# A decoder trunk on one core: the weights' low parts of the first pair of chunks and of two down-projection pairs are made by other engines, at other places

## The chip, the cores and the metric

The kernel runs on one core of a Trainium2 chip. The metric is the device time of one execution in microseconds; here it is the median of 3 runs, 1110.24 us (1109.77 to 1112.19). Lower is better. The profile is of one further execution, which took 1109.46 us; between the first and the last instruction that it shows lie 1107.7 us.

## The reference, cut to what matters

512 positions of width 1024 pass through two decoder layers: one with dilated sliding-window attention, one with forgetting attention, and after each attention a gated convolutional feed-forward network (FFN) of width 2816. All is in float32. The change touches only the FFN:

```python
def conv_ffn(xn, w_up, cw, cb, w_down):
    a = xn @ w_up                                   # 1024 -> 2 * 2816
    ap = jnp.pad(a, ((0, 0), (CONV_W - 1, 0), (0, 0)))
    a = sum(ap[:, j:j + T] * cw[j] for j in range(CONV_W)) + cb
    gate, val = jnp.split(a, 2, axis=-1)
    return (jax.nn.gelu(gate, approximate=True) * val) @ w_down
```

## The kernel before

**Splits.** TensorE multiplies in a rounded float32 format. To keep float32 precision, each operand is split in a high part (a cast) and a low part (the operand less its high part), and each product is three matmuls: high times high, high times low, low times high (`mm3`, lines 294 to 297; L295, L296 and L297 in the profile). So each weight tile of 128x1024 (512 KB, called `wraw` when loaded by the SP queue, L48) must be split before TensorE can use it. The high part is always a cast on ScalarE. The low part is made in one of three ways: `low` subtracts on VectorE (L740, L76, L837) or, with an argument, on GpSimd; `added` has ScalarE write the negative of the high part's tile (L743: a copy of the raw tile with scale -1 into the rounded format) and then GpSimd issue a transfer that adds the raw tile to it (L744). The transfer reads the raw tile until it has landed.

**The up-projection** goes by chunks of 128 gate and 128 value columns, 22 chunks. The chunks 4 to 19 go in eight pairs, `PAIRS = range(2, 10)`. A pair is computed by a scheme with seven products instead of eight (sums and differences of blocks of weights and of the input are multiplied). TensorE takes the products of a pair in the order A11, S2, S3, A12, S1, A22, S4, with the next pair's A11 between A22 and S4. Each product is 24 matmuls (2 column halves, 4 blocks, 3 parts). VectorE adds products in PSUM between them: `sums` (L1062, "csum") and `ends` (L1047, L1048).

The generator `prepare(p)` (L730) makes the seven weight operands of a pair. Each `next(steps)` in the main loop (L1053 and on) lets it go one step further, so the order of its steps against the loop's own lines is the order of the instructions in each engine's queue. `ga`, `va`, `vb` and `gb` are the four raw tiles of a pair. `s3` and `s2` are differences of them. `gb` is A12's operand as it is; later GpSimd overwrites it with `gb - s2` (L782), and that is S4's operand. For the first pair (p = 2) the low parts of A11, S3, A12, S1, A22 and S4 are all made by `added`; for the later ones A11, S2 and S3 are done by VectorE, A12 by GpSimd, S1, A22 and S4 by `added`. In the loop the rest of the pair's generator is run after S2's product (`for _ in steps: pass`): that rest is S4's cast and `added`. Then the next pair's generator begins with the cast of its A11, later its low part.

After S2's product `sums(s12, ...)` waits to read what S2 wrote, and A12's product writes to the same PSUM bank, so A12's first matmul waits for that addition. `keep_first` (L1040) copies A11's result to SBUF for the same sums.

After a chunk's products come bias (L657 or L670), two convolution taps (L664, VectorE), GELU (L689), the product of gate and value on GpSimd (L686, "hc"), and a transfer of the result to DRAM (L684).

**The down-projection** takes 11 pairs of the 22 chunks, also by a scheme with fewer products. Its operands are two weight tiles and one tile of activations (`dact`) per pair. `pair_sums` (L823 to L825) forms sums of activations, `pair_highs` casts the three tiles (L833), `pair_lows` subtracts (L837), and `mul_one` issues the matmuls ("acc"), which multiply in the order activation high by weight high, activation high by weight low, activation low by weight high. The preparation of pairs 0 to 2 is placed among the last chunks of the up-projection; `down` begins with the highs of pair 3.

Of the kernel before, what the change touches and what calls it, by code (L numbers as in the profile page):

```python
# [12 lines left out]
AF = mybir.ActivationFunctionType  # L13
ALU = mybir.AluOpType
# [13 lines left out]
PAIRS = range(2, 10)  # L28
# [87 lines left out]
def trunk_kernel(ctx, tc, x, norm_gains, w_qkv_a, w_o_a, w_q_b, w_o_b, kv_norm, w_kvf, b_f,  # L116
                 w_up, conv_w, conv_b, w_down, rope, out):
    nc = tc.nc
    act, dve, pool, pe, sp = nc.scalar, nc.vector, nc.gpsimd, nc.tensor, nc.sync
# [529 lines left out]
    def ffn(l, bd, cp, nxt, ahead):  # L649
# [11 lines left out]
        def shifted(c, banks, bb, s):  # L661
            ps, ch = banks[s], s * NF + c
            for n in (1, 2):
                dve.scalar_tensor_tensor(bb[:, s, n:], ps[:, :T - n], cp[:, 2 - n, ch:ch + 1], bb[:, s, n:],  # L664
                                         ALU.mult, ALU.add)
# [22 lines left out]
        def glu(c, bb):  # L688
            act.activation(bb[:, 0, :], bb[:, 0, :], AF.Gelu_apprx_tanh)  # L689
            gated.append((c, bb))  # L690

        def post(c, banks, between=None):
            product()
            glu(c, taps(c, banks, between))
# [35 lines left out]
        def prepare(p):  # L730

            first = p == PAIRS[0]

            def high(a, raw):
                w[a] = t8([128, 2, 1024], F32R, name="w")
                act.copy(w[a][:, 0], raw)  # L736
                W2[p, a] = w[a].rearrange("p s (k c) -> p s k c", k=4)

            def low(a, raw, engine=dve):
                engine.tensor_tensor(w[a][:, 1], raw, w[a][:, 0].bitcast(F32), ALU.subtract)  # L740

            def added(a, raw):
                act.activation(w[a][:, 1], raw, AF.Copy, scale=-1.0)  # L743
                pool.dma_start(w[a][:, 1], raw, accum_op=ALU.add)  # L744

            w = {}
            ga = grab(2)
            high("A11", ga)
            if first:
                added("A11", ga)  # L750
            yield
            if not first:
                low("A11", ga)
            yield
            va = grab(1)
            s3 = t4([128, 1024], name="wsum")
            dve.tensor_tensor(s3, ga, va, ALU.subtract)
            high("S3", s3)
            if first:
                added("S3", s3)  # L760
            yield
            vb = grab(1)
            dve.tensor_tensor(va, va, vb, ALU.add)
            yield
            s2 = t4([128, 1024], name="wsum") if first else ga
            dve.tensor_tensor(s2, va, ga, ALU.subtract)  # L766
            high("S2", s2)
            gb = grab(1)
            high("A12", gb)
            if first:  # L770
                added("A12", gb)
            yield
            low("S2", s2)
            if not first:
                low("A12", gb, pool)
            high("S1", va)
            added("S1", va)
            W.load(W.n_split + 2)
            yield
            if not first:  # L780
                low("S3", s3)
            pool.tensor_tensor(gb, gb, s2, ALU.subtract)  # L782
            high("A22", vb)
            added("A22", vb)
            W.load(W.n_split + 3)
            yield
            high("S4", gb)
            added("S4", gb)
            yield
# [15 lines left out]

        acts, one, two, raws, later2 = {}, {}, {}, {}, {}
        H = slice(0, 512), slice(512, 1024)
        a11, s1_, s3_, s2_ = (slice(i * 256, i * 256 + 256) for i in range(4))  # L810

# [13 lines left out]
            dve.tensor_tensor(k[:, s2_], k[:, s1_], k[:, a11], ALU.subtract)  # L825
            pool.dma_start(sD[j], k[:, s2_])

        def pair_highs(j):

            raws[j] = [*W.take(2), acts.pop(j)]  # L830
            one[j] = [t8([128, 2, 1024], F32R, name="w") for _ in range(3)]
            for w, r in zip(one[j], raws[j]):
                act.copy(w[:, 0], r)  # L833

        def pair_lows(j):
            for w, r in zip(one[j], raws.pop(j)):
                dve.tensor_tensor(w[:, 1], r, w[:, 0].bitcast(F32), ALU.subtract)  # L837

        def load_two(j):
# [150 lines left out]
        first = first_products(bd, 3)  # L990
# [12 lines left out]
        steps = prepare(PAIRS[0])  # L1003
# [48 lines left out]
        s1 = keep_first(banks)  # L1052
        for p in PAIRS:  # L1053
            nxt_steps = prepare(p + 1) if p + 1 in PAIRS else prepare_last()
            if p + 1 not in PAIRS:
                pair_load(0)
            o2, o3, o4 = [[b[i][:, h] for b in banks] for i, h in ((0, HI), (1, LO), (1, HI))]
            s17, s12 = (t2([128, 2, 256], name="csum") for _ in range(2))

            def sums(dst, os, src):  # L1060
                for q in range(2):
                    dve.tensor_tensor(dst[q] if isinstance(dst, list) else dst[:, q], os[q], src[:, q], ALU.add)  # L1062

            times(p, "S2", o2)
            ends(pend)
            for _ in steps:
                pass
            steps = nxt_steps
            next(steps)
            bbs = [biased(*pend[0][:2])]  # L1070
            if p + 1 in PAIRS:
                next(steps)
            times(p, "S3", o3, True)
            sums(s12, o2, s1)
            bbs += [biased(*e[:2]) for e in pend[1:]]
            product()
            next(steps)
            shifted(*pend[0][:2], bbs[0], 0)
            times(p, "A12", [b[0][:, LO] for b in banks])
            sums(s17, o3, s1)  # L1080
            next(steps)
            shifted(*pend[0][:2], bbs[0], 1)
            glu(pend[0][0], bbs[0])
            times(p, "S1", o2)
            product()
            next(steps)
            if len(pend) > 1:
                shifted(*pend[1][:2], bbs[1], 0)
            times(p, "A22", o3)
            sums(o4, o2, s17)  # L1090
            next(steps)
            if len(pend) > 1:
                shifted(*pend[1][:2], bbs[1], 1)
                glu(pend[1][0], bbs[1])
            if p + 1 in PAIRS:
                later = begin(p + 1)
            else:
                W.n_get += 4 * len(PAIRS)
                begun = W.get(), bank([128, T], name="up")
                up(*begun, range(4))  # L1100
            next(steps, None)
            times(p, "S4", o2)
            pend = [(2 * p + q, banks[q], q, s1, s12) for q in range(2)]
            if p + 1 in PAIRS:
                banks, s1 = later, keep_first(later)
# [6 lines left out]
        ends(pend)  # L1112
        product()
        glu(pend[0][0], taps(*pend[0][:2]))
        pair_highs(1)
        up(W.get(), banks[1], range(KD))
        post(*pend[1][:2])
        pair_sums(2)
# [4 lines left out]
        glu(before[0], taps(*before, lambda: pair_lows(1)))  # L1123
        up(W.get(), banks[1], range(KD))
        before = NF - 1, banks
        post(*before)
        pair_highs(2)
        pair_sums(3)
        pair_lows(2)
        product()  # L1130
        pool.dma_start(hD[NF - 1], hc.pop(NF - 1))

# [513 lines left out]
    first, second = bd2.order[:2], bd2.order[2:]  # L1646
# [212 lines left out]
    for n in range(N + 3):  # L1859
        live = n < N  # L1860
        if live:
            j, i = units[n]
# [98 lines left out]
```

## Time and profile before

| | |
|---|---|
| median of 3 runs | 1110.24 us (1109.77 to 1112.19) |
| the profiled execution | 1109.46 us |
| its span, first to last instruction | 1107.7 us |
| mean granted clock of TensorE | 0.994 |
| TensorE busy | 1084.8 us (98%) |
| VectorE busy | 886.9 us (80%) |
| ScalarE busy | 699.7 us (63%) |
| GpSimd busy | 316.4 us (29%) |

A row of the timeline gives start, duration, engine, line of the code, operation, and what is written from what; in brackets the engine's idle time before it and what ended that. Engines: PE is TensorE, DVE is VectorE, ACT is ScalarE, POOL is GpSimd, SPq the queue of SP, which issues most loads. A row of the list of waits gives who waited for whom: microseconds in total, how many times, the longest. A row of the chain gives start, length and what the time went to. A row of the windows gives the stretch, its length, the busy time of PE, of weight loads, DVE, ACT and POOL, then TensorE's granted clock as a share of full speed, the share of the DMA engines' time, and GB/s. The two FFNs run the same code; the first pair of chunks lies near 222 us and near 806 us.

### The profile page before, as it was taken

The page shows a single profiled execution, that of the slowest core. Times are in us where ns is not written, and L with a number is a line of the kernel's source. Part 1 is how long each engine was busy: PE and PEld are TensorE (multiplying, and loading weights), DVE is VectorE, ACT ScalarE, POOL GpSimd, SP SyncE. Part 2 cuts the span into 40 slices and gives each one's busy share as a digit, 9 for nine tenths or more (in the row PEclk, how much of TensorE's full clock was granted, in tenths as well). Part 3 has the DMA queues.
Part 4 walks back from the last instruction along what each step waited for, and adds up shares of the span by engine and source line. Part 5 has one row for each costly group of instructions (what it writes and reads, how often), then busy time and mean ns, then how long its engine had stood idle before and what let it go on. Part 6 is the DMA issues. An engine that isn't in the chain of part 4 may idle for free.

```text
span 1107.7 us, 18966 instructions
## 1 busy us (share of the span) xinstructions
PE 1084.8 (98%) x6897; PEld 961.5 (87%) x6897; DVE 886.9 (80%) x1446; ACT 699.7 (63%) x1151; POOL 316.4 (29%) x334
## 2 busy tenths in 40 slices
PE   9999999979999999999999999999979999999997
PEld 7888889879999987888888888889879999987886
DVE  5898978459899889997686667868538889889995
ACT  6745767747676647576451678756757577656573
POOL 3543000355565531000001211100345466522000
PEclk9999999989999999999999999999989999999999
DMA  9799956988888978893447857766888878978962
GB/s 293 242 368 406 345 125 153 188 200 191 230 194 213 256 241 284 301 338 100 152 133 255 266 163 222 259 196 159 172 210 189 217 200 200 244 241 288 347 248 76
DMA packets 162101, 252.15 MB, mean 228 GB/s; under 512 B 13152, under 2 KB 106712, under 8 KB 162008
## 3 DMA queue, kind: packets, MB, share of 16 engines
q1 hardware_dynamic: 143784, 189.33, 51.5%
q0 software_dynamic: 17536, 61.61, 25.1%
q8 instruction: 54, 0.88, 0.3%
q14 instruction: 39, 0.32, 0.1%
q10 hardware_dynamic: 688, 0.01, 0.0%
HBM read 172.37 MB, written 39.73 MB: 191 GB/s over the span
## 4 chain that ended last, share of the span: by engine, by line
PE 87%; DMA 4%; issue 3%; POOL 2%; DVE 2%; ACT 1%; SPq 0%; DVEq 0%; ACTq 0%; POOLq 0%
PE up L295 11%; PE up L297 11%; PE up L296 11%; PE acc L297 8%; PE acc L295 8%; PE acc L296 8%; PE v_ps L295 2%; PE v_ps L296 2%; PE v_ps L297 2%; PE pT_ps L1802 2%; PE o_ps L1817 2%; DMA w<-wraw 2%; PE s_ps L1768 2%; PE first L297 1%; PE qk_ps L295 1%
## 5 line engine op out<-in xcount | busy, mean ns | idle before, releaser
L295 PE MATMUL up<-xsh,w 128*128 128x256 f32 x512 | 145.5, 284 | 1.0 <-ACT csum L1040 1.0
L736 ACT CAST w<-wraw 128x1024 fp32r<-128x1024 f32 x94 | 95.3, 1042 | 80.9 <-DVE wraw L766 41.1
L297 PE MATMUL up<-xsh,w 128*128 128x256 f32 x512 | 145.2, 284 | 0.0
L296 PE MATMUL up<-xsl,w 128*128 128x256 f32 x512 | 145.2, 284 | 0.0
L664 DVE SCALAR_TENSOR_TENSOR bb<-up,conv,bb 128x511 f32<-128x511 f32 (+1 forms) x160 | 118.4, 745 | 21.5 <-ACT bb L670 18.6
L297 PE MATMUL acc<-w 128*128 128x512 f32 (+1 forms) x311 | 120.7, 388 | 3.3 <-DVE w L837 3.3
L295 PE MATMUL acc<-w 128*128 128x512 f32 (+1 forms) x311 | 120.7, 388 | 0.0
L686 POOL TENSOR_TENSOR hc<-bb 128x512 f32<-128x512 f32 x44 | 77.3, 1757 | 98.7 <-DVE bb L664 76.5
L296 PE MATMUL acc<-w 128*128 128x512 f32 (+1 forms) x267 | 103.3, 387 | 0.0
L295 PEld LDWEIGHTS up<-xsh,w 128*128 128x128 f32 x512 | 98.7, 193 | 1.4 <-ACT csum L1040 1.4
L296 PEld LDWEIGHTS up<-xsl,w 128*128 128x128 f32 x512 | 98.6, 193 | 0.0
L297 PEld LDWEIGHTS up<-xsh,w 128*128 128x128 f32 x512 | 98.6, 192 | 0.0
L295 PE MATMUL up<-xch,w 128*128 128x256 f32 (+1 forms) x256 | 80.6, 315 | 6.0 <-DVE csum L1062 6.0
L295 PE MATMUL up<-xbh,w 128*128 128x256 f32 (+1 forms) x256 | 80.3, 313 | 5.3 <-DVE csum L1062 5.3
L296 PE MATMUL up<-xcl,w 128*128 128x256 f32 (+1 forms) x256 | 80.4, 314 | 0.0
L297 PE MATMUL up<-xch,w 128*128 128x256 f32 (+1 forms) x256 | 80.4, 314 | 0.0
L296 PE MATMUL up<-xbl,w 128*128 128x256 f32 (+1 forms) x256 | 80.0, 313 | 0.0
L297 PE MATMUL up<-xbh,w 128*128 128x256 f32 (+1 forms) x256 | 80.0, 312 | 0.0
L740 DVE TENSOR_TENSOR w<-wraw,w 128x1024 fp32r<-128x1024 f32 x28 | 46.8, 1671 | 37.7 <-ACT w L736 37.7
L76 DVE TENSOR_TENSOR w<-wraw,w 128x1024 fp32r<-128x1024 f32 x50 | 60.2, 1222 | 18.4 <-ACT w L58 14.2
L58 ACT CAST w<-wraw 128x1024 fp32r<-128x1024 f32 x61 | 62.9, 1059 | 17.9 <-PE v_ps L296 6.9
L297 PEld LDWEIGHTS acc<-w 128*128 128x128 f32 x311 | 58.4, 188 | 16.0 <-DVE w L837 4.2
(314 smaller groups left out, 3191.2 us busy)
## 6 DMA issues: line engine op xcount, KB each, us to landing
wraw<-in_w_up_dram SPq DMA_DIRECT2D x88, 512.0 KB
w<-wraw POOLq DMA_DIRECT2D x64, 512.0 KB, 5.3
dT<-dsums SPq DMA_DIRECT2D x28, 512.0 KB
dsums<-in_w_down_dram SPq DMA_DIRECT2D x22, 512.0 KB
dsums<-in_w_down_dram SPq DMA_DIRECT2D x44, 256.0 KB
hD<-hc POOLq DMA_DIRECT2D x44, 256.0 KB, 6.2
dact<-hD SPq DMA_DIRECT2D x44, 256.0 KB
wraw<-dT SPq DMA_DIRECT2D x22, 512.0 KB
```

The lines of the kernel that those rows point to most:

```text
L58: (copy or self.nc.scalar.copy)(pair[:, 0], raw)
L76: self.nc.vector.tensor_tensor(pair[:, 1], raw, pair[:, 0].bitcast(F32), ALU.subtract)
L295: pe.matmul(o, ah, bh, start=first, stop=False, skip_group_check=shared)
L296: pe.matmul(o, ah, bl, start=False, stop=False, skip_group_check=shared)
L297: pe.matmul(o, al, bh, start=False, stop=last, skip_group_check=shared)
L664: dve.scalar_tensor_tensor(bb[:, s, n:], ps[:, :T - n], cp[:, 2 - n, ch:ch + 1], bb[:, s, n:], ALU.mult, ALU.add)
L686: pool.tensor_tensor(hc[c], bb[:, 0, :], bb[:, 1, :], ALU.mult)
L736: act.copy(w[a][:, 0], raw)
L740: engine.tensor_tensor(w[a][:, 1], raw, w[a][:, 0].bitcast(F32), ALU.subtract)
L1768: pe.matmul(sc[j, i][hh][:, :nn], qT[j][own, qp, i * 128:(i + 1) * 128], k[own, kp, :nn], start=qp + kp == 0, stop=qp == 1)
L1802: pe.transpose(o[:, k0 + k, :], p[:, hh, k * 128:(k + 1) * 128], ident)
L1817: pe.matmul(o[64 * hh:64 * hh + 64, i * 128:(i + 1) * 128], Vt[hd // 8][:, k, (hd % 8) * 64:(hd % 8) * 64 + 64], pT[j, i, hh][:, k, :], st ...
```

## The change

There are four edits, and they act once in each of the two FFNs.

1. In the first pair, the low parts of S3 and A12 are made by VectorE (`low`) and no longer by ScalarE and a transfer.
2. In the first pair, S4's cast and `added` are no longer run right after S2's product. The generator is kept as `ready` and is run on after A12's product and the sums and step behind it.
3. `pair_highs(1, True)` and `pair_highs(2, True)`: for the down-projection's second and third pair (1 and 2) ScalarE writes the negatives of the two weight tiles and GpSimd issues adding transfers; `pair_lows` then subtracts only for the tile of activations (`todo`).
4. `pair_highs(2)` is moved ahead of the last chunk's `post`, and `pair_lows(2)` ahead of `pair_sums(3)`.

```diff
@@ -756,8 +756,6 @@
             s3 = t4([128, 1024], name="wsum")
             dve.tensor_tensor(s3, ga, va, ALU.subtract)
             high("S3", s3)
-            if first:
-                added("S3", s3)
             yield
             vb = grab(1)
             dve.tensor_tensor(va, va, vb, ALU.add)
@@ -767,18 +765,14 @@
             high("S2", s2)
             gb = grab(1)
             high("A12", gb)
-            if first:
-                added("A12", gb)
             yield
             low("S2", s2)
-            if not first:
-                low("A12", gb, pool)
+            low("A12", gb, dve if first else pool)
             high("S1", va)
             added("S1", va)
             W.load(W.n_split + 2)
             yield
-            if not first:
-                low("S3", s3)
+            low("S3", s3)
             pool.tensor_tensor(gb, gb, s2, ALU.subtract)
             high("A22", vb)
             added("A22", vb)
@@ -805,7 +799,7 @@
 
 
 
-        acts, one, two, raws, later2 = {}, {}, {}, {}, {}
+        acts, one, two, raws, todo, later2 = {}, {}, {}, {}, {}, {}
         H = slice(0, 512), slice(512, 1024)
         a11, s1_, s3_, s2_ = (slice(i * 256, i * 256 + 256) for i in range(4))
 
@@ -825,15 +819,20 @@
             dve.tensor_tensor(k[:, s2_], k[:, s1_], k[:, a11], ALU.subtract)
             pool.dma_start(sD[j], k[:, s2_])
 
-        def pair_highs(j):
+        def pair_highs(j, added=False):
 
             raws[j] = [*W.take(2), acts.pop(j)]
             one[j] = [t8([128, 2, 1024], F32R, name="w") for _ in range(3)]
             for w, r in zip(one[j], raws[j]):
                 act.copy(w[:, 0], r)
+                if added and r is not raws[j][2]:
+                    act.activation(w[:, 1], r, AF.Copy, scale=-1.0)
+                    pool.dma_start(w[:, 1], r, accum_op=ALU.add)
+            todo[j] = slice(2 if added else 0, 3)
 
         def pair_lows(j):
-            for w, r in zip(one[j], raws.pop(j)):
+            s = todo.pop(j)
+            for w, r in zip(one[j][s], raws.pop(j)[s]):
                 dve.tensor_tensor(w[:, 1], r, w[:, 0].bitcast(F32), ALU.subtract)
 
         def load_two(j):
@@ -1063,9 +1062,9 @@
 
             times(p, "S2", o2)
             ends(pend)
-            for _ in steps:
-                pass
-            steps = nxt_steps
+            ready, steps = steps, nxt_steps
+            if p != PAIRS[0]:
+                next(ready)
             next(steps)
             bbs = [biased(*pend[0][:2])]
             if p + 1 in PAIRS:
@@ -1079,6 +1078,8 @@
             times(p, "A12", [b[0][:, LO] for b in banks])
             sums(s17, o3, s1)
             next(steps)
+            if p == PAIRS[0]:
+                next(ready)
             shifted(*pend[0][:2], bbs[0], 1)
             glu(pend[0][0], bbs[0])
             times(p, "S1", o2)
@@ -1112,7 +1113,7 @@
         ends(pend)
         product()
         glu(pend[0][0], taps(*pend[0][:2]))
-        pair_highs(1)
+        pair_highs(1, True)
         up(W.get(), banks[1], range(KD))
         post(*pend[1][:2])
         pair_sums(2)
@@ -1123,10 +1124,10 @@
         glu(before[0], taps(*before, lambda: pair_lows(1)))
         up(W.get(), banks[1], range(KD))
         before = NF - 1, banks
+        pair_highs(2, True)
         post(*before)
-        pair_highs(2)
+        pair_lows(2)
         pair_sums(3)
-        pair_lows(2)
         product()
         pool.dma_start(hD[NF - 1], hc.pop(NF - 1))
 
```

Neither TensorE's order nor SP's order changes. What stands in other queues, at three places, follows. Line numbers of the changed kernel differ a little (L1062 is L1061, L833 is L827, L837 is L836; its L829 is the new activation).

ScalarE's queue from A12's cast in the first FFN's first pair; tile 2279 is `gb` (A12's operand, then S4's), 2183 is S1's, 2225 A22's, and 2322 the next pair's A11. Before:

```order
L736 CAST w_2324<-wraw_2279 128x1024
L743 ACTIVATE w_2324<-wraw_2279 128x1024
L689 ACTIVATE bb_2311<-bb_2311 128x512
L736 CAST w_2330<-wraw_2183 128x1024
L743 ACTIVATE w_2330<-wraw_2183 128x1024
L736 CAST w_2361<-wraw_2225 128x1024
L743 ACTIVATE w_2361<-wraw_2225 128x1024
L1040 COPY csum_2395<-up_2367 128x256
L1040 COPY csum_2395<-up_2369 128x256
L736 CAST w_2424<-wraw_2279 128x1024
L743 ACTIVATE w_2424<-wraw_2279 128x1024
L736 CAST w_2428<-wraw_2322 128x1024
```

Now, from A22's cast on (`gb` is tile 2277, the next A11's raw 2320, S3's operand of the next pair wsum_2457):

```order
L736 CAST w_2359<-wraw_2225 128x1024
L743 ACTIVATE w_2359<-wraw_2225 128x1024
L1039 COPY csum_2393<-up_2365 128x256
L1039 COPY csum_2393<-up_2367 128x256
L736 CAST w_2422<-wraw_2320 128x1024
L657 ACTIVATE bb_2424<-up_2280,conv_1644 128x512
L657 ACTIVATE bb_2424<-up_2281,conv_1644 128x512
L736 CAST w_2459<-wsum_2457 128x1024
L736 CAST w_2492<-wraw_2277 128x1024
L743 ACTIVATE w_2492<-wraw_2277 128x1024
```

The next pair's A11 cast comes right behind the copies; S4's two operations follow behind the bias activations and the next pair's S3 cast.

VectorE's queue at the same place, from `s2` (L766) to the next pair's `s3` (L757). Before:

```order
L766 TENSOR_TENSOR wsum<-wraw 128x1024
L740 TENSOR_TENSOR w<-wsum,w 128x1024
L740 TENSOR_TENSOR w<-wraw,w 128x1024
L1062 TENSOR_TENSOR csum<-up,csum 128x256 x2
L757 TENSOR_TENSOR wsum<-wraw 128x1024
```

Now:

```order
L764 TENSOR_TENSOR wsum<-wraw 128x1024
L740 TENSOR_TENSOR w<-wsum,w 128x1024
L740 TENSOR_TENSOR w<-wraw,w 128x1024
L740 TENSOR_TENSOR w<-wsum,w 128x1024
L740 TENSOR_TENSOR w<-wraw,w 128x1024
L1061 TENSOR_TENSOR csum<-up,csum 128x256 x2
L757 TENSOR_TENSOR wsum<-wraw 128x1024
```

The two L740 rows before are the low parts of S2 and of the next pair's A11; A12's and S3's now stand between them. The additions that release A12's product (csum) still stand behind the next A11's low part.

ScalarE's queue at the end of the up-projection: the bias activations and GELU of chunk 20, then of chunk 21, and the highs of pair 2 and of pair 3. Before:

```order
L670 ACTIVATE bb<-up,conv 128x512 x2
L689 ACTIVATE bb<-bb 128x512
L670 ACTIVATE bb<-up,conv 128x512 x2
L689 ACTIVATE bb<-bb 128x512
L833 CAST w<-wraw 128x1024 x2
L833 CAST w<-dact 128x1024
```

Now:

```order
L670 ACTIVATE bb<-up,conv 128x512 x2
L689 ACTIVATE bb<-bb 128x512
L827 CAST w<-wraw 128x1024
L829 ACTIVATE w<-wraw 128x1024
L827 CAST w<-wraw 128x1024
L829 ACTIVATE w<-wraw 128x1024
L827 CAST w<-dact 128x1024
L670 ACTIVATE bb<-up,conv 128x512 x2
L689 ACTIVATE bb<-bb 128x512
L827 CAST w<-wraw 128x1024 x2
```

Pair 2's highs, with two activations more, now stand ahead of chunk 21's bias and GELU.

## The prediction

> **What bounds the kernel now.** I read the page first (the span, the engines' busy time and the costliest groups), then the list of TensorE's waits, then the chain of work that ended last around the longest wait, and last the engines' timelines there.
>
> ```profile
> span 1107.7 us, 18966 instructions
> PE 1084.8 (98%) x6897; PEld 961.5 (87%) x6897; DVE 886.9 (80%) x1446; ACT 699.7 (63%) x1151; POOL 316.4 (29%) x334
> ```
> ```profile
> PE up L295 <- DVE csum L1062: 11.3, 2, 6.0
> PE acc L297 <- DVE w L837: 3.3, 2, 1.7
> PE up L295 <- ACT csum L1040: 1.0, 2, 0.5
> ```
>
> TensorE is busy for 98%, so only its waits, and what they do to its clock, can be won back without taking matmuls away. The change takes none away. Three kinds of wait, each twice (once per FFN), make nearly all of the list. Here are the two longest with what follows them, and the clock there:
>
> ```profile
> 221.22 0.28 PE L297 MATMUL up<-xbh,w 128*128 128x256 f32 x1
> 222.00 0.39 PE L295 MATMUL up<-xsh,w 128*128 128x256 f32 x1 [0.50 <-ACT csum L1040]
> ...
> 227.74 0.28 PE L297 MATMUL up<-xsh,w 128*128 128x256 f32 x1
> 233.33 0.58 PE L295 MATMUL up<-xbh,w 128*128 128x256 f32 x1 [5.31 <-DVE csum L1062]
> ...
> 237.72 0.28 PE L297 MATMUL up<-xbh,w 128*128 128x256 f32 x1
> 237.84 0.28 PE L295 MATMUL up<-xsh,w 128*128 128x256 f32 x1
> ```
> ```profile
> 811.64 0.28 PE L297 MATMUL up<-xsh,w 128*128 128x256 f32 x1
> 817.89 0.58 PE L295 MATMUL up<-xch,w 128*128 128x256 f32 x1 [5.97 <-DVE csum L1062]
> ...
> 823.17 0.42 PE L295 MATMUL up<-xsh,w 128*128 128x256 f32 x1
> ```
> ```profile
> 233.30:235.00 1.70, 1.67 (x8) 1.67 (x9) 1.70 (x2) 0.00 (x0) 1.37 (x2) 0.50 1.05 207
> 237.00:238.00 1.00, 1.00 (x11) 1.00 (x10) 1.00 (x2) 0.33 (x1) 0.00 (x0) 1.00 0.94 291
> 422.60:424.60 2.00, 1.98 (x9) 1.64 (x10) 1.83 (x4) 1.37 (x2) 0.47 (x1) 1.00 0.45 119
> ```
>
> In the windows the number behind the engines is the granted clock. After the 5.31 us wait it is 0.50, and at 237 us 1.00 again; after the wait of 1.72 us (below) it stays 1.00. So a long wait is paid twice, a short one once. Matmuls at full clock start 0.12 apart (237.72, 237.84), so one product of 24 takes 2.88 us. Losses, start to start: in the first FFN S2 0.66 (222.00−221.22−0.12); A12 5.47 (233.33−227.74−0.12) and 1.63 more in the product (237.84−233.33−2.88). In the second FFN A12 6.13 and 2.40 (823.17−817.89−2.88). S1 begins slow there too (0.42 at 823.17 instead of 0.28), an estimated 0.3 over three or four matmuls.
>
> Why does A12 wait? The chain from the late transfer to the first matmul, with start and length:
>
> ```profile
> 217.69 8.52 DMA w<-wraw
> 226.35 2.38 POOL wraw L782
> ...
> 229.70 1.05 ACT w L743
> 230.75 0.94 ACT w L736
> ...
> 232.86 0.43 DVE csum L1062
> ```
> ```profile
> 231.72 1.22 DVE L740 TENSOR_TENSOR w<-wraw,w 128x1024 fp32r<-128x1024 f32 x1 [14.98 <-ACT w L736]
> 801.58 9.19 DMA w<-wraw
> ```
>
> A12's accumulating transfer reads its raw tile; L782 (gb−=s2, on GpSimd) overwrites that tile and waits 8.52 us for it (9.19 in the second FFN). ScalarE's S4 cast waits for L782, and in its queue behind S4 stands the next pair's A11 cast. VectorE, idle for 14.98 us, waits for that cast with its A11 low, and behind this low in its queue stands csum, which releases A12. So A12 waits for a split that it doesn't need, through three queues.
>
> **The change part by part.** *A12 and S3 on VectorE.* Per FFN two ScalarE activations and two transfers go, and two lows come.
>
> ```profile
> L740 DVE TENSOR_TENSOR w<-wraw,w x3: 1224/1227/2497, 231.7 to 251.9; 128x1024 fp32r<-128x1024 f32 x3
> 214.43 1.05 ACT L736 CAST w<-wsum 128x1024 fp32r<-128x1024 f32 x1 [3.50 <-DVE wsum L766]
> ...
> 220.65 1.05 ACT L743 ACTIVATE w<-wraw 128x1024 fp32r<-128x1024 f32 x1
> ```
>
> Two lows are 2×1.23 us in a stretch in which VectorE idles for 14.98: nothing on the path. A12's cast follows S2's, so ends at about 215.5 (one S3 activation less before 214.43 also moves it 0.95 forward); S2's, A12's and S3's lows end at about 215.7, 216.9 and 218.0. L782 then runs from about 218.7 (behind S1's transfer on GpSimd) to 221.1 instead of to 228.7. ScalarE's last activation before csum's copies (220.65) ends about 1.9 earlier, at 219.8, so the first copy isn't late and S2's 0.66 goes; the second FFN has the same wait (1.0 in 2).
>
> *S4 two products later.* The next A11 cast comes right behind the copies, at about 221.9 to 222.9; A11's low 224.2; csum needs S2's product (221.34+2.88=224.2) and ends at about 225.1. A12 is due at 221.34+2×2.88=227.1. Margin 2.0; if a GpSimd tensor operation stretches that low to 2.50 it is 0.7. So A12 waits for nothing, and with no wait of 5 us its clock stays 1.00. Gain: 5.47+1.63+0.66=7.76 and 6.13+2.40+0.3+0.66=9.49, together 17.3.
>
> What is late next? S4's cast and activation now run behind S3's cast of the next pair. That one needs VectorE's subtraction behind csum (225.1, and 1.2 like a low: 226.3), so the three operations of some 0.95 end at about 229.2, and the transfer is issued. S4 is the seventh product from S2: due at 221.34+6×2.88=238.6, 9.4 us later.
>
> ```profile
> DMA to landing us min/median/max: 4.5/5.3/9.3
> ```
>
> Over all the transfers of L744 the longest landing is 9.3, the median 5.3. I take no wait; the bounds are 0 and, if such a transfer is once more behind another, some 3 us each.
>
> *The down-projections.* Here VectorE is late, TensorE waits in the third matmul of pair 2:
>
> ```profile
> 420.52 0.39 PE L296 MATMUL acc<-w 128*128 128x512 f32 x1
> 422.62 0.50 PE L297 MATMUL acc<-w 128*128 128x512 f32 x1 [1.72 <-DVE w L837]
> ```
> ```profile
> 407.31 3.59 DVE L837 TENSOR_TENSOR w<-wraw,w 128x1024 fp32r<-128x1024 f32 x2
> ...
> 411.96 4.41 DVE L664 SCALAR_TENSOR_TENSOR bb<-up,conv,bb 128x511 f32<-128x511 f32 x6
> ...
> 417.54 3.90 DVE L837 TENSOR_TENSOR w<-wraw,w 128x1024 fp32r<-128x1024 f32 x2
> ```
> ```profile
> 409.61 0.78 ACT L670 ACTIVATE bb<-up,conv 128x512 f32<-128x512 f32 x1 [0.82 <-PE up L297]
> 415.02 0.63 ACT L689 ACTIVATE bb<-bb 128x512 f32<-128x512 f32 x1 [4.63 <-DVE bb L664]
> 415.56 1.98 ACT L833 CAST w<-wraw 128x1024 fp32r<-128x1024 f32 x2
> ```
>
> Loss: 422.62−420.52−0.23=1.87, in the second FFN some 1.75. VectorE is rid of 3.59 and 3.90 us. But chunk 21's taps now stand behind five ScalarE operations of pair 2 (three casts, two activations, 0.95 each): these run from about 409.9, when GELU of chunk 20 is free, to 414.7, so the tap activations that ran by 409.61 end at about 416.1, VectorE's taps at 418.4 and pair 2's only low at 419.6. It is due at 420.75: no wait. Its two transfers are issued at about 411.9 and 413.8, due at 420.5 and 421.2: room for 8.6 and 7.4, between the median 5.3 and the longest 9.3.
>
> Then the sums of pairs 3 and 4 (six of 0.43) and pair 3's lows, which end at about 425.4, due at 426.3. What speaks against it:
>
> ```profile
> 390.47 2.74 DVE L837 TENSOR_TENSOR w<-wraw,w 128x1024 fp32r<-128x1024 f32 x1
> 390.82 1.30 POOL L686 TENSOR_TENSOR hc<-bb 128x512 f32<-128x512 f32 x1
> ```
>
> A low beside GpSimd's hc took 2.74 instead of 1.21. Chunk 21's hc would begin near 422, beside pair 3's first low; then the lows end at 426.8, and mul_one(3) waits 0.5. The Trainium skill, "SBUF — State Buffer", section "Who interferes with whom", says that a VectorE instruction with two SBUF inputs and a GpSimd one that reads SBUF exclude each other; these two rows agree with it. By that rule the overlap is sure and the gain 1.3 per FFN; by cover alone it would be 1.8. I take 1.05 per FFN, between 0 (one of these steps 2 us late) and 1.8: 2.1 in both. Pair 1's two transfers are issued near 400 and 402 and due from 412.0 on (420.3−12×0.69), so they cost nothing themselves; the 1.9 us that ScalarE pays for them before chunk 19's taps fall into VectorE's freed 3.59. But they stand on GpSimd's queue ahead of chunk 18's hc, and behind that hc SP holds a load for pair 2:
>
> ```profile
> 399.06 1.29 POOL L686 TENSOR_TENSOR hc<-bb 128x512 f32<-128x512 f32 x1 [6.07 <-DVE bb L664]
> ```
> ```profile
> 400.38 0.32 SPq L48 DMA_DIRECT2D wraw<-dT  x1
> ```
>
> This load goes out at about 404.7 instead of 400.38, and pair 2's second cast wants it at 411.8 (409.9+2×0.95): 7.1 us of room. If it lands later, chunk 21's taps and pair 2's low behind that cast come later by as much, and the low has only 1.1 us to spare (419.6, due 420.75); one more reason to take less than 1.8.
>
> Sum: 17.3+2.1−0=19.4, against the profiled run of 1109.46 us (span 1107.7): 1090.1. The median is 1110.24, 0.8 more, so 1090.8 us.
>
> **The rivals.** (1) *S4 is waited for instead of A12.* The removed wait was just such a transfer, 8.5 and 9.2 us long with others close before it. For it: S4's transfer now starts when TensorE has 9.4 us left. Against: the queue ahead of it is emptier by two transfers, and A22's is issued 8 us before. It decides from 9.4 us to landing; at 12.4 it costs 3 us per FFN: 1096.8, or, with one FFN alone, 1093.8. Chance 0.15.
>
> (2) *The wait in the down-projections is as long as before, in another place.* For it: chunk 21's taps end 2.0 us later than now (418.4 for 416.4), the transfers' room is only 2 to 3 us over the median, and a load goes out 4 us later. Against: VectorE has 7.5 us less to do. Then nothing comes from there: 1092.9. Chance 0.08.
>
> (3) *The chain is not broken:* something else holds the A11 cast or csum until about 233 (its buffer, its raw tile). For it: csum's place in the queue is still behind A11's low. Against: at 231.72 this low waited for ScalarE alone. Only S2 and the down part gain, 3.4 us: 1106.8, or no difference if these don't come either. Chance 0.04.
>
> (4) *Slower: transfers of GpSimd starved in the down part.* The place is pair 2 at mul_one(2): VectorE is nearly without rest there, and if its operations keep GpSimd from getting the transfers out, TensorE waits until VectorE pauses, and beyond about 5 us pays the half clock with some 2.4 more. Without any wait there the time would be 1089.3 (1110.24−17.3−3.6), and each FFN adds its wait and the 2.4. Above 1112.4 it takes waits of 9.2 us, that is a landing 17.8 us after the issue (8.6+9.2); at 20 us it would be 1116.9. Against: the longest of all is 9.3, in stretches with VectorE as busy. The Trainium skill, "SBUF — State Buffer", section "SBUF: two separate sides", warns of just this trap for transfers issued from GpSimd, though for VectorE's two-port modes; no row of this trace shows a starved one. Chance 0.04.
>
> **How the numbers follow.** The forecast (all of the first pair, some of the down part) has 0.69: 1088.5 (all 17.3 and all 3.6 of the down part, less the 0.8 by which the profiled run and the median differ) to 1092.9. Rival 1 reaches to 1096.8 and a little on, rival 2 ends at 1092.9. The range is 1088.5 to 1096.5; outside are rivals 3 and 4 and the end of rival 1. About 0.2% (2.2 us) is what a measurement of this kernel can tell from no change. Faster: 0.69+0.15+0.08+half of rival 3=0.94; I say 0.93; same 0.03; slower 0.04.
>
> **What would show it.** Right: no wait of TensorE for csum, neither DVE's nor ACT's, near 227 and 800 us; L782 ending near 221; VectorE's A11 low no longer behind 15 us of idling; the clock at 1.00 through A12; the span shorter by about 17 before the down part of the second FFN. Wrong: a new wait at S4 for a transfer w<-wraw; a wait at mul_one(2) or mul_one(3) of over 2 us; a mean clock below 0.994, which would mean that TensorE without rests is granted less.

## The result and the profile after

| | before | after |
|---|---|---|
| median | 1111.22 us (4 runs, 1109.77 to 1113.77) | 1095.05 us (4 runs, 1093.60 to 1095.57) |
| ratio after to before | | 0.985 (95% interval 0.9827 to 0.9873) |
| span of the profiled execution | 1107.7 us | 1093.8 us |
| mean granted clock of TensorE | 0.994 | 0.997 |

The change gains 16.2 us in the medians and 13.9 us in the two profiles; the forecast was 19.4. The page after, its first two lines, and the list of TensorE's waits:

```profile
span 1093.8 us, 18994 instructions
PE 1082.7 (99%) x6897; PEld 958.0 (88%) x6897; DVE 888.1 (81%) x1442; ACT 703.5 (64%) x1155; POOL 320.7 (29%) x338
```
```profile
PE acc L295 <- DVE bb L664: 3.1, 4, 1.5
PE warm L249 <- DVE zero L244: 1.2, 1, 1.2
PE acc L296 <- DMA w<-wraw: 0.5, 1, 0.5
PE acc L297 <- DVE w L836: 0.3, 1, 0.3
```

Both waits for csum, VectorE's and ScalarE's, are gone. In their place stand four for L664 (the taps) at the down-projections, which were not there before. First the first pair, TensorE's timeline (S2 begins at 221.36, A12 at 227.12, S1 at 230.00), then GpSimd's and VectorE's rows there:

```profile
221.24 0.28 PE L297 MATMUL up<-xbh,w 128*128 128x256 f32 x1
221.36 0.28 PE L295 MATMUL up<-xsh,w 128*128 128x256 f32 x1
...
227.00 0.28 PE L297 MATMUL up<-xsh,w 128*128 128x256 f32 x1
227.12 0.28 PE L295 MATMUL up<-xbh,w 128*128 128x256 f32 x1
...
230.00 0.28 PE L295 MATMUL up<-xsh,w 128*128 128x256 f32 x1
```
```profile
218.86 2.68 POOL L776 TENSOR_TENSOR wraw<-wraw,wsum 128x1024 f32<-128x1024 f32 x1
...
222.39 1.89 POOL L686 TENSOR_TENSOR hc<-bb 128x512 f32<-128x512 f32 x1
230.69 0.87 POOL L744 DMA_DIRECT2D w<-wraw  x1 [6.42 <-issue]
```
```profile
222.91 2.46 DVE L740 TENSOR_TENSOR w<-wraw,w 128x1024 fp32r<-128x1024 f32 x1 [4.82 <-ACT w L736]
225.29 0.74 DVE L1061 TENSOR_TENSOR csum<-up,csum 128x256 f32<-128x256 f32 x2
```

L776 (the old L782) runs at 218.9 instead of 226.3. The next A11's low starts at 222.9 instead of 231.7; GpSimd's hc at 222.4 stretches it to 2.46, as the prediction's tighter case had it, and csum is still done at 226.0, 1.1 us before A12 is due. Matched matmul by matmul, the first pair gains 7.9 us in the first FFN and 9.6 in the second (forecast 7.8 and 9.5). S4's transfer goes out at 230.7 and holds up nobody.

Now the down-projections. TensorE's rows with a wait in the first FFN, then in the second; VectorE's and ScalarE's rows in the first; the windows of the second (the number ahead of the last two is the granted clock):

```profile
409.17 0.47 PE L295 MATMUL acc<-w 128*128 128x512 f32 x1 [0.65 <-DVE bb L664]
...
410.61 0.47 PE L295 MATMUL acc<-w 128*128 128x512 f32 x1 [0.50 <-DVE bb L664]
...
415.72 0.50 PE L296 MATMUL acc<-w 128*128 128x512 f32 x1 [0.52 <-DMA w<-wraw]
```
```profile
987.40 0.47 PE L295 MATMUL acc<-w 128*128 128x512 f32 x1 [1.46 <-DVE bb L664]
...
988.84 0.47 PE L295 MATMUL acc<-w 128*128 128x512 f32 x1 [0.51 <-DVE bb L664]
```
```profile
404.79 1.05 ACT L829 ACTIVATE w<-wraw 128x1024 fp32r<-128x1024 f32 x1
405.75 1.04 ACT L827 CAST w<-dact 128x1024 fp32r<-128x1024 f32 x1
406.69 1.43 ACT L670 ACTIVATE bb<-up,conv 128x512 f32<-128x512 f32 x2
```
```profile
407.49 2.98 DVE L664 SCALAR_TENSOR_TENSOR bb<-up,conv,bb 128x511 f32<-128x511 f32 x4 [2.31 <-ACT bb L670]
```
```profile
985.50:989.00 3.50, 1.54 (x6) 0.70 (x6) 3.21 (x5) 2.50 (x5) 1.62 (x2) 1.00 1.08 285
989.00:994.00 5.00, 5.00 (x16) 3.94 (x16) 4.86 (x9) 3.75 (x5) 1.73 (x3) 0.66 1.05 284
```
```profile
L830 POOL DMA_DIRECT2D w<-wraw x8: 872/890/908, 392.4 to 984.4; - x8
...
DMA to landing us min/median/max: 4.6/6.8/9.5
```

ScalarE's five operations of pair 2 end at 406.8, chunk 21's bias follows, VectorE has idled 2.31 us and ends chunk 21's taps at 410.5 (`x4` from 407.49, 2.98 long). The second half of `mul_one(0)` writes its last two products to the PSUM banks that these taps read; TensorE waits for them at 409.17 and 410.61. At 415.72 it waits once more, for one of pair 2's transfers. The old wait of 1.7 us at `mul_one(2)` is gone, and what came for it is as long or longer: the down part loses 0.5 us in the first FFN and 2.7 in the second instead of gaining 1.05 each (17.5−3.3, less 0.3 between the FFNs, are the 13.9). Of the 2.7, about 1.5 are a clock of 0.66 of full speed over 5 us behind waits of 1.46 and 0.51 us. Other executions of the same kernel had mean clocks of 1.0 and 0.998 and took 1093.60 and 1094.53 us, against 1095.56 of the profiled one. A second profile of the same kernel (E9, below) has the same waits of 1.46 and 0.50 us without the fall of the clock; there the down part loses 0.0 and 1.8 us.

### The profile page after: what moved, and what is told of

Same layout as the page of the kernel before. It is cut to its first block, busy times and chain, and to the rows that moved or that the text cites. A ratio compares the mean times of both kernels' runs of the same rounds, so it can differ in the third digit from the quotient of the medians.

```text
span 1093.8 us, 18994 instructions
## 1 busy us (share of the span) xinstructions
PE 1082.7 (99%) x6897; PEld 958.0 (88%) x6897; DVE 888.1 (81%) x1442; ACT 703.5 (64%) x1155; POOL 320.7 (29%) x338
## 4 chain that ended last, share of the span: by engine, by line
PE 90%; DMA 3%; issue 2%; ACT 2%; DVE 2%; POOL 1%; SPq 0%; DVEq 0%; ACTq 0%; POOLq 0%
PE up L295 11%; PE up L297 11%; PE up L296 11%; PE acc L295 8%; PE acc L297 8%; PE acc L296 8%; PE v_ps L295 2%; PE v_ps L296 2%; PE v_ps L297 2%; PE pT_ps L1803 2%; PE o_ps L1818 2%; PE s_ps L1769 2%; PE qk_ps L295 1%; PE first L295 1%; PE first L296 1%
## 5 line engine op out<-in xcount | busy, mean ns | idle before, releaser
L664 DVE SCALAR_TENSOR_TENSOR bb<-up,conv,bb 128x511 f32<-128x511 f32 (+1 forms) x160 | 118.6, 746 | 28.0 <-ACT bb L670 25.2
L295 PE MATMUL up<-xch,w 128*128 128x256 f32 (+1 forms) x256 | 79.3, 310 | 0.0
L297 PE MATMUL up<-xch,w 128*128 128x256 f32 (+1 forms) x256 | 79.3, 310 | 0.0
L76 DVE TENSOR_TENSOR w<-wraw,w 128x1024 fp32r<-128x1024 f32 x50 | 60.1, 1221 | 17.6 <-ACT w L58 13.3
L58 ACT CAST w<-wraw 128x1024 fp32r<-128x1024 f32 x61 | 62.8, 1054 | 17.5 <-PE v_ps L296 6.9
L295 PEld LDWEIGHTS acc<-w 128*128 128x128 f32 x311 | 58.8, 189 | 16.4 <-issue 2.9
L297 PEld LDWEIGHTS acc<-w 128*128 128x128 f32 x311 | 58.8, 189 | 12.8 <-DVE w L836 0.7
```

Source lines behind the costliest of these rows:

```text
L58: (copy or self.nc.scalar.copy)(pair[:, 0], raw)
L76: self.nc.vector.tensor_tensor(pair[:, 1], raw, pair[:, 0].bitcast(F32), ALU.subtract)
L295: pe.matmul(o, ah, bh, start=first, stop=False, skip_group_check=shared)
L297: pe.matmul(o, al, bh, start=False, stop=last, skip_group_check=shared)
```

## The experiments

Time is given against the kernel before in the same series of runs, since that one's median was 1111.2 to 1113.2 from series to series. E1 to E4 ran in one series (before: 1113.15), E5 to E8 in the next (1112.12), E9 to E12 in the last (1112.53).

**E1: edits 1 and 2 alone.** The lines are against the changed kernel, as in the later diffs.

```diff
-        pair_highs(1, True)
+        pair_highs(1)
...
-        pair_highs(2, True)
         post(*before)
-        pair_lows(2)
+        pair_highs(2)
         pair_sums(3)
+        pair_lows(2)
```

> Edits 1 and 2 alone (the first pair); the down-projections' pairs as before. Theory: the whole gain comes from the first pair (17.5 us in the profiles, start to start), and edits 3 and 4 lose some 3.3 us against it because chunk 21's bias activations stand behind pair 2's highs, so that the PSUM banks which the first down products take are free late. Then this kernel runs in 1110.2-17.4 = 1092.8 us, 2 us faster than the changed kernel, and the waits of 1.7 and 1.6 us at mul_one(2) for VectorE are back. Rival: edits 3 and 4 are neutral or a gain of their own, and the first pair gives less in undisturbed runs than in the profile: 1095 to 1097 us.

1094.86 us, 18.3 less than before (ratio 0.9831, 0.981 to 0.9851). Its waits:

```profile
PE acc L297 <- DVE w L836: 3.2, 2, 1.6
PE pT_ps L1803 <- ACT prob L1781: 1.3, 1, 1.3
```

The old waits at `mul_one(2)` are back, the first pair gains 7.9 and 9.6, and the span is 1091.9 us, below the changed kernel's 1093.8, though a wait of 1.3 us is new in the second layer's attention (below). So the whole gain is the first pair's, and edits 3 and 4 together lose a little. The median alone would not tell: it lies between the theory's 1092.8 and the rival's 1095, since the kernel before, too, took 2.9 us more in this series than the figure that both were reckoned from. E9 and E11, the same two kernels on one chip, confirm it (1094.53 and 1093.48 us, without an overlap of their runs).

**E2: edit 1 alone, and E3: edit 2 alone.** E2 runs S4's steps at the old place (`for _ in steps: pass`), E3 gives S3 and A12 back to `added` in the first pair; edits 3 and 4 are undone in both.

> Edit 1 alone (S3's and A12's lows by VectorE); S4's two operations stay right behind S2's product. Theory: either cut breaks the chain, since L782 no longer waits for a transfer and ends near 221, S4's cast and activation end near 223.8, the next A11's low at 226.1, csum at 226.9, and A12 is due at 227.1: no wait, 1092.8 us. Rival: both cuts are needed; with S4 still ahead of the next A11 on ScalarE csum is late by 1 to 2 us in each FFN: 1095 to 1097 us.

> Edit 2 alone (S4's operations two products later); S3's and A12's lows stay with ScalarE and transfers. Theory: csum is released without S4; A12's transfer lands near 226.2, before A12 at 227.8; L782 then runs to 228.7, S4's transfer is issued near 231.3 and lands 6.8 later, before S4 is due at 239.3. Only the wait of 0.5 us for the copies (L1040) stays, 0.66 us per FFN: 1094.1 us. Rival: the late transfer now holds A12 itself or S4 for 2 to 3 us per FFN: 1098 to 1100 us.

E2 took 1099.49 us (13.7 less than before), E3 1103.89 (9.3 less). VectorE in E2 where csum is made, and TensorE's waits in E3:

```profile
224.83 1.23 DVE L740 TENSOR_TENSOR w<-wraw,w 128x1024 fp32r<-128x1024 f32 x1 [6.71 <-ACT w L736]
225.98 0.75 DVE L1061 TENSOR_TENSOR csum<-up,csum 128x256 f32<-128x256 f32 x2
```
```profile
PE acc L297 <- DVE w L842: 4.9, 3, 2.0
PE up L297 <- DMA w<-wraw: 3.5, 3, 1.6
PE up L295 <- DVE csum L1067: 2.5, 4, 0.7
```

In E2 csum ends at 226.7, TensorE waits for none of the first pair, and matched matmul by matmul the profile shows all of the 17.5 us there (7.9 and 9.6). The expectation of E12, below, says 17.1; but the 0.35 us that E2 loses in the first FFN are at `mul_one(1)`, far behind the first pair. So VectorE's lows alone break the chain. That E2 is 4.6 us above E1 is not in the first pair: its waits at `mul_one(2)` are 2.0 us instead of 1.6, and the clock falls behind them (some 1.6 us in each FFN). Why these waits are longer than E1's was not tried. In E3 A12 no longer waits for csum, but L782 (the line's number in E3 as before) still waits 5.8 us for A12's transfer, GpSimd's queue is late behind it, and TensorE waits for the transfers of A22 and S4 instead (0.35 and 1.54 us in the first FFN, 1.59, A22's, in the second). So the rival's kind of wait came, though not at A12, and E3 is some 4 us slower than the rival said: its first pair gains only 4.7 and 7.0, and the four waits for csum in later pairs (told of at the end) cost its profile some 3.6.

**E4: edits 1 and 2, and edit 3 for pair 1 alone** (`pair_highs(1, True)` kept, the rest as E1).

> Edits 1 and 2, and edit 3 for pair 1 alone; pair 2's highs and lows stand where they stood before and its lows are VectorE's. Theory (the place of pair 2's highs is the fault): chunk 21's banks are free in time, VectorE begins pair 2's lows some 2.4 us earlier than before, and the waits at mul_one(2) of 1.7 and 1.6 us go without a new one: 1110.2-17.4-3.6 = 1089.2 us. Rival (the extra activations and transfers themselves are the fault): the waits at the first down products stay as in the changed kernel, 1 to 3 us per FFN: 1093 to 1096 us.

1097.26 us, 15.9 less than before, 2.4 more than E1. This speaks against my theory, which expected 1089: freeing VectorE of pair 1's lows gains next to nothing. The rows that show it are VectorE's at chunk 19's taps (it idled 2.83 us there in the kernel before) and at pair 1's one remaining low, the activations'; E4's waits stand behind them:

```profile
395.70 2.98 DVE L664 SCALAR_TENSOR_TENSOR bb<-up,conv,bb 128x511 f32<-128x511 f32 x4 [4.74 <-ACT bb L670]
...
401.29 2.50 DVE L836 TENSOR_TENSOR w<-dact,w 128x1024 fp32r<-128x1024 f32 x1
```
```profile
PE acc L297 <- DVE w L836: 4.7, 3, 2.0
PE up L295 <- DVE csum L1061: 2.5, 4, 0.7
```

The 1.9 us that ScalarE spends on the negatives become idle time of VectorE, and the remaining low, now the one beside GpSimd's hc, takes 2.50 us instead of the 1.21 of before. That leaves some 0.4 of the 3.59 that VectorE was freed of, so the wait at `mul_one(2)` in the first FFN falls only from 1.60 to 1.35. The rival isn't borne out either: its waits at the first down products, for the taps, are not in the list. So I formed theory A: edit 3 is the loss, through ScalarE; edit 4 by itself is a gain. E4's time alone doesn't show the first half: in its profile the four waits for csum, in later pairs of the second FFN (told of at the end), cost some 3.6 us, and longer waits at that FFN's `mul_one(1)` and `mul_one(2)`, with the clock behind the second, some 3.8.

**E5: edits 1, 2 and 4, without edit 3** (`pair_highs(1)` and `pair_highs(2)` without `True`, the order as changed). **E6: the changed kernel with pair 2's highs behind chunk 21's taps. E7: edits 1 and 2 and only the lows of pair 2 moved** (pair 1's highs are without `True` there, a line that the diff leaves out).

```diff
E6:
-        pair_highs(2, True)
-        post(*before)
+        product()
+        bb = taps(*before)
+        pair_highs(2, True)
+        glu(before[0], bb)
E7:
-        pair_highs(2, True)
         post(*before)
+        pair_highs(2)
         pair_lows(2)
```

> Edits 1, 2 and 4, without edit 3: pair 2's three casts stand ahead of chunk 21's bias and its lows ahead of pair 3's sums, but no negatives and no adding transfers for pairs 1 and 2. Theory A (edit 3 is the fault: five ScalarE operations ahead of chunk 21's bias, and two ahead of chunk 19's, make VectorE wait for ScalarE): with three casts the bias ends at 404.6 in a profile with the first pair's gain, while VectorE is busy to 405.7, so no bank is late; the lows of pair 2 run from 408.7 to 412.2 and are due near 412.9, so the waits of 1.7 and 1.6 us go: 21 us less than the kernel before on the same chip (17.5 and 3.6). Theory B (the move itself is the fault): the banks are still late, waits for L664 at the first down products of 0.5 to 1.5 us: 16 to 18 us less than before.

> The changed kernel with pair 2's highs (with negatives and transfers) between chunk 21's taps and its GELU, instead of ahead of the bias. Theory A: the waits for L664 (late PSUM banks) go, but the two transfers are issued near 405.4 and 407.3 and, at the 8.5 and 9.5 us that they took in the changed kernel, land at 413.9 and 416.8 with 412.7 and 413.4 due; TensorE waits 1 to 3.4 us per FFN for w<-wraw: 14 to 18 us less than the kernel before. Theory B (only the place was the fault): no wait is left, 21 us less.

> Edits 1 and 2, and of edit 4 only that pair 2's lows stand ahead of pair 3's sums; its highs stand behind chunk 21's post as before. Theory A: pair 2's lows begin 1.3 us earlier, and GpSimd's hc of chunk 21, which stands behind pair 3's sums in its queue, no longer lies beside them (one took 2.76 us there); they run from 408.9 to 412.5, due near 412.9: the waits at mul_one(2) go, 20 to 21 us less than the kernel before. Theory B: the three sums are only moved behind, and pair 3's lows are late instead by 1 to 2 us: 17 to 18 us less.

E5 took 1092.15 us, 20.0 less than before; E6 1104.99, 7.1 less; E7 1092.91, 19.2 less. E5's list of waits and its ScalarE and VectorE; E6's list and its clock; E7's list:

```profile
PE acc L297 <- DVE w L836: 1.4, 2, 0.7
```
```profile
400.32 1.98 ACT L827 CAST w<-wraw 128x1024 fp32r<-128x1024 f32 x2
402.21 1.05 ACT L827 CAST w<-dact 128x1024 fp32r<-128x1024 f32 x1
403.16 1.44 ACT L670 ACTIVATE bb<-up,conv 128x512 f32<-128x512 f32 x2
```
```profile
404.26 4.40 DVE L664 SCALAR_TENSOR_TENSOR bb<-up,conv,bb 128x511 f32<-128x511 f32 x6
408.58 2.35 DVE L836 TENSOR_TENSOR w<-wraw,w 128x1024 fp32r<-128x1024 f32 x2
410.85 1.22 DVE L836 TENSOR_TENSOR w<-dact,w 128x1024 fp32r<-128x1024 f32 x1
```
```profile
PE acc L296 <- DMA w<-wraw: 9.2, 4, 3.0
```
```profile
418.00:424.00 6.00, 4.88 (x12) 3.82 (x13) 5.90 (x9) 1.99 (x2) 0.95 (x2) 0.50 1.03 395
```
```profile
PE acc L297 <- DVE w L836: 2.1, 2, 1.0
```

In E5 the same move has no late bank: with three casts chunk 21's bias ends at 404.6, before VectorE gets to its taps, which end at 408.7. Pair 2's two weight lows run undisturbed in 2.35 us instead of 3.90, and nothing waits at `mul_one(2)`; 0.7 us is left at `mul_one(3)` in each FFN. The time lies between what the two theories said (21 and 16 to 18 us less); the rows decide: theory A's mechanism holds, theory B's late banks are not there. So the banks are late only with both edits, the place of edit 4 and the two activations of edit 3 in it. E6 shows the other half: with the banks in time the two transfers themselves are late, as theory A said, but by more: TensorE waits 9.2 us for them in all, where 2 to 7 were expected, the clock goes to 0.50, and 7.1 us are gained instead of 14 to 18. E7 lies between its two theories, and each has a part: the waits at `mul_one(2)` go, and two of 1.0 us come at `mul_one(3)`, for pair 3's lows. So moving the lows alone brings more than half of what edit 4 brings: 0.6 and 0.5 us in the two down-projections of its profile, against 1.0 and 0.9 in E5's.

**E8: as E5, with S4's steps later in all eight pairs** (`next(ready)` after A12 without its `if`).

> As e5, and S4's cast and added run two products later in all eight pairs, not only in the first. In two of the profiles so far TensorE waited 0.3 to 0.7 us for csum in each of four later pairs, where GpSimd's low of A12 took 3.4 us instead of 2.4 beside a VectorE low; S4's cast waits for GpSimd's L776 behind it, and the next A11's cast, its low and csum stand behind S4's. Theory: with S4 later csum hangs on GpSimd no more, no execution has these waits, S4's transfers still land some 3 us before they are due, and the time is that of e5 or up to 3 us less, with less spread. Rival: the later transfers collide with the next pair's and S4 or A22 is waited for: 1 us or more per pair, 8 to 16 us more than e5.

1093.20 us, 18.9 less than before; E5 is 1.1 below it, with overlapping runs. No pair waits for csum, and none for S4, but no such wait was in E5's profile either; neither the expected gain nor the rival's loss shows.

**E9 to E12: four kernels on one chip.** E9 is the changed kernel, E10 is E5, E11 is E1, E12 is E5 with edit 2 undone.

> The changed kernel once more, beside the next three on one chip. Theory A (edit 3 loses, edits 1, 2 and 4 gain): slowest of the four, some 16 us less than the kernel before. Rival (the differences between the earlier kernels are those between chips and executions): all four within 1 us of each other.

> Edits 1, 2 and 4 without edit 3, once more. Theory A: the fastest of the four, 20 us less than the kernel before, 3 to 4 us less than the changed kernel. Rival: as the changed kernel.

> Edits 1 and 2 alone, once more. Theory A: between the two, 17 to 18 us less than the kernel before: the waits of 1.6 us at mul_one(2) are back, each some 1.9 us against the kernel with edit 4. Rival: as the changed kernel.

> Edits 1 and 4, with S4's operations right behind S2's product as before (edit 2 undone). In the profile with edit 1 alone the first pair gained 17.1 of the 17.5 us. Theory: VectorE's lows alone break the chain, and this kernel is within 1 us of the one with edits 1, 2 and 4. Rival: edit 2 is needed in undisturbed executions, since the kernel with edit 1 alone took 4.6 us more than the one with both: 3 to 5 us more here too.

| kernel | median, us | lowest to highest | less than before |
|---|---|---|---|
| E9: changed | 1094.53 | 1094.22 to 1095.33 | 18.0 |
| E10: edits 1, 2, 4 | 1092.32 | 1091.84 to 1094.96 | 20.2 |
| E11: edits 1, 2 | 1093.48 | 1093.13 to 1093.63 | 19.1 |
| E12: edits 1, 4 | 1094.43 | 1093.25 to 1095.06 | 18.1 |

The order is the one that theory A gave, with smaller steps: 2.2 us between E10 and E9, 1.2 between E10 and E11. One run of E10 (1094.96) lies among E9's, so the 2.2 us are near what these runs can tell; but E5 and E1, the kernels of E10 and E11, had stood 20.0 and 18.3 below their series' kernel before, and the changed kernel 16.2 in the first measurement, so the order is the same there. E9 and E11 differ by 1.05 us, and their runs don't overlap: edits 3 and 4 together lose. E10, with 20 us less than before in both series, is the best version found. E12 is 2.1 us above E10, more than the theory's 1 and less than the rival's 3, with overlapping runs. None of it is in the first pair: that gains 7.9 and 9.6 in E12's profile as in E10's. So whether edit 2 is worth anything stays open.

## Why the prediction was right in the first pair and wrong in the down-projections

- *The chain over L782, S4, A11 and csum.* Right, with its sizes: 17.3 forecast, 17.5 measured. E2 shows that the first cut, at A12's transfer, does all of it by itself; the second adds nothing to it that the profiles show. E3 shows that the second cut alone only moves the wait on to A22 and S4.
- *S4 next in line.* Right: no wait, with the transfer out at 230.7 (forecast 229.2) and 238.6 due. Waits of rival 1's kind, 1.54 us at most, came only in E3, where edit 1 was missing.
- *The down part, +2.1 forecast, −3.3 measured (−0.5 and −2.7).* The step that failed: "VectorE's taps at 418.4 and pair 2's only low at 419.6. It is due at 420.75: no wait." The delay of the taps was worked out, and it came, but I asked only when pair 2's low would be done, and not who else waits for chunk 21's taps. The first down products do, for the banks: they waited 0.65 and 0.50 us in the first FFN, 1.46 and 0.51 in the second. Rival 2 (chance 0.08) named the delayed taps, and a wait as long as before in another place is what came; but it let the down part come to nothing, and not to a loss. None of the stated signs of being wrong showed, since they named `mul_one(2)`, `mul_one(3)` and S4, and not `mul_one(0)`. In E9's execution, where the clock did not fall, the down part lost 1.8 us and not 3.3.
- *VectorE's freed time.* "the 1.9 us that ScalarE pays for them before chunk 19's taps fall into VectorE's freed 3.59" is so, but little is left of the 3.59: 1.9 went into a longer wait for ScalarE (4.74 us idle in E4) and 1.3 into the stretch beside hc, which passed to the remaining low (2.50 us). Edit 3 takes work from an engine that was itself waiting for ScalarE, and gives more to ScalarE.
- *The transfers' landing.* I took the median of L744's landings, 5.3 us, as the likely one. Of L830's eight the longest took 9.5 us; pair 2's in the first FFN, where the DMA engines' share was 1.05 and more, took 8.5 and 9.5, and TensorE waited 0.52 us for one.
- *The price of a wait.* "a long wait is paid twice, a short one once", with the border at some 5 us, was wrong: 1.46 and 0.51 us in a row cost 1.5 us more in the profiled execution, and nothing more in E9's.

That the forecast and the time still lie close together is due to the first pair, which is 17.3 of the forecast's 19.4 us. That 1095.05 us lies within the stated range is in part luck: the forecast without its rivals ended at 1092.9, and it was rival 1, a wait at S4, that had stretched the range to 1096.5. That wait did not come, and the wait for the banks, which the range did not provide for, took its place; besides, the kernel before took 1.0 us more in the measurement of the change than the median that the forecast went by.

## What to carry to other kernels

When an engine's operation is delayed, list everyone who waits for it: the reader of its result, and also the next writer of the buffer that it reads. Before work is taken off an engine, look at what ended that engine's idle time: VectorE here was waiting for ScalarE, and more work went to ScalarE. The long chain over three queues here was cut by its oldest link alone, the transfer that kept a tile occupied (E2); the cut further down alone moved the wait elsewhere (E3).

## What the runs showed of the hardware

- **The clock falls after shorter waits than thought.** No fall after single waits of 1.60 and 1.72 us; a fall after 1.46 and 0.51 in a row, and after single ones of 2.01 (E2) and 2.00 (E4, some 1.6 us lost), but not after 2.00 in E3, nor after 1.46 and 0.50 in a row in E9. So the length of the wait alone does not decide; what else does was not tried. The Trainium skill, "TensorE: Matmul & The Clock Gate", Part 1, "What's actually happening", gives an idle window of about 3.4 us; these falls came after less idle time than that.
- **Two lasting states of one race.** In the later pairs GpSimd makes A12's low beside a VectorE low. GpSimd and VectorE in the second FFN, first in E1, then in E4:

```profile
893.44 2.43 POOL L740 TENSOR_TENSOR w<-wraw,w 128x1024 fp32r<-128x1024 f32 x1 [1.00 <-ACT w L736]
```
```profile
894.71 2.23 DVE L740 TENSOR_TENSOR w<-wraw,w 128x1024 fp32r<-128x1024 f32 x1
```
```profile
893.76 3.36 POOL L740 TENSOR_TENSOR w<-wraw,w 128x1024 fp32r<-128x1024 f32 x1 [1.01 <-ACT w L736]
```
```profile
893.62 1.22 DVE L740 TENSOR_TENSOR w<-wraw,w 128x1024 fp32r<-128x1024 f32 x1
```

In these rows whichever starts first is done in its own time (2.43 and 1.22 us), and the other is stretched by about 1 us. In E3 and E4 VectorE came first in four pairs running, S4's cast was late behind L776 (E3's L782), and each pair waited 0.3 to 0.7 us for csum. The Trainium skill, "SBUF — State Buffer", "Who interferes with whom", says that the order of issue decides who is blocked; the two pairs of rows agree. The prediction's pair beside hc does not, by its recorded starts: VectorE's low began first (390.47 against 390.82) and was the one stretched, to 2.74 us.
- **A wait far away that comes and goes.** In the second layer's attention TensorE waited 1.3 to 1.7 us for ScalarE's L1781 in E1, E2, E5, E7, E8, E10, E11 and E12, the kernels with two GpSimd transfers per FFN fewer than before, and not before, in the changed kernel (also E9), E4 or E6; E3, with as many transfers as before, has one of 0.2. So, if the transfers are the cause, part of what edit 3 loses in the down part it has back there. In E5's trace VectorE's operation ahead of it starts when a GpSimd transfer (L96) lands; why two transfers in another stage should shift that was not tried and stays open.
